# Two busiest experts in groups of 32 rows, token lists made at the second layers, projection weights in wider parts

## The chip, the cores and the metric

The kernel runs on one core of one Trainium2 chip. The metric is the time of one execution in microseconds of device time, given as the median of several runs.

## What is computed

Two transformer blocks follow each other on 256 tokens of width 1024, in fp32. The first has a mixer (convolution and two kinds of attention) and a mixture of 32 experts, of which each token goes to 4. The second has two layers of attention and feed-forward over the same tokens and a context of 256 more. The change lies in the experts and in how projection weights are loaded everywhere. The experts' part of the reference:

```python
logits = (xt @ router_w + router_b).astype(jnp.float32)
top_vals, top_idx = lax.top_k(logits, TOP_K)
top_w = jax.nn.softmax(top_vals, axis=-1)
combine = jnp.einsum('tk,tke->et', top_w, one_hot(top_idx, N_EXPERTS))

def expert_step(acc, params):
    w1, b1, w2, b2, gate_e = params
    u = xt @ w1 + b1
    glu = jnp.minimum(u[:, ::2], SWIGLU_LIMIT)
    lin = jnp.clip(u[:, 1::2], -SWIGLU_LIMIT, SWIGLU_LIMIT)
    a = glu * jax.nn.sigmoid(SWIGLU_ALPHA * glu) * (lin + 1)
    out = a @ w2 + b2
    return acc + gate_e[:, None] * out, None
```

## The kernel before

The program has three stages: the first block's mixer (0 to 266 us in the profile), the experts (to about 1597 us), and the latent layers of the second block. While the experts run, a second stream of work, the *side stream*, is fed in between: the layers of the second block that need only the context. `along` gives it credit at each step of an expert; `SHARE` says how much, by the expert's size.

The experts are sorted by their number of tokens and run in that order. Each has a fixed room (`CAPS`): 128 rows for the two busiest (ranks 0 and 1), 64 for ranks 2 to 17, 32 for the rest. What does not fit would be done in a loop at the end. From rank 2 on, the first layer of the next expert stands ahead of the second layer of this one. An expert does the following.

- Its tokens are gathered by matmuls with a 0/1 matrix (`held`, `inward`, L858).
- `first` (bias L887 or L889, matmuls L899) multiplies the tokens by 8 weight pieces of 1 MB (`m_raw`, from `in_w_mlp` on SP's queue, five buffers). For 128 rows each 512 columns are done as two tiles of 64 rows, for 64 rows as one, for 32 rows as one of 32; such tiles run side by side on the array.
- `act` (L909 to L916) is the gated activation, a chain that alternates between VectorE (DVE) and ScalarE (ACT), in the tiles `glu` and `sg`, which have one buffer each. `across` (L924) transposes its result, and ScalarE copies it to `aT`.
- `second` (L957) multiplies by 4 more pieces. `halved` (L966, L967) scales the result by each row's gate and splits it in a high and a low part.
- `scatter` (L1007) brings the rows back to their tokens: matmuls with `selT`, a 0/1 matrix made from the expert's token list, added to the output on VectorE (`add`, L981). One scatter serves one expert of 128 rows, or a pair of smaller ones.

The lists of tokens and gates of all 32 experts are made before the first scatter by `ranked`, in 16 rounds of two experts. A round compares each token's place in the expert with the row number (L789, two operations on VectorE), multiplies by token number and gate (L794, four matmuls), and puts the result in `lists` and `gates` (L796 to L799).

All other projections go through `Weights` with `w_raw`, `w_hi`, `w_lo`. A piece of 2048 columns is loaded in `PIECES` parts. ScalarE rounds a part to `w_hi` (L96); VectorE or GpSimd (POOL) subtracts to get `w_lo` (L98): GpSimd takes each sixth part in the first mixer, all beside the experts, and each second in the latent layers (`POOL_EVERY`); then three matmuls (L195, L196, L197) use them. `LEAD` is how many parts are split ahead, `LAG` by how many parts loading trails the splitting. Beside the experts the ACT queue loads these parts, in the latent layers the SP queue does (both by L113).

## Time and profile before

| | |
|---|---|
| Time, median of 3 runs | 2373.54 us (2371.75 to 2374.51) |
| Profiled execution | 2361.89 us, span 2360.2 us, mean granted clock 0.957 |
| TensorE (PE) busy | 2137.9 us, 91% of the span |
| VectorE (DVE) busy | 1135.5 us, 48% |
| ScalarE (ACT) busy | 892.8 us, 38% |
| GpSimd (POOL) busy | 625.1 us, 26% |
| DMA | 667.5 MB, mean 283 GB/s |
| Experts' weights | 384 pieces of 1 MB on SP's queue, median 8.1 us from issue to landing |

The shares are averages over three stages that differ. In the page's 40 slices the DMA engines are at nine tenths or more for most of the experts' stage, and TensorE in the latent layers and at the start of the experts. So a stretch is to be read before an average.

### The profile page before, as it was taken

The page shows a single profiled execution, that of the slowest core. Times are in us where ns is not written, and L with a number is a line of the kernel's source. Part 1 is how long each engine was busy: PE and PEld are TensorE (multiplying, and loading weights), DVE is VectorE, ACT ScalarE, POOL GpSimd, SP SyncE. Part 2 cuts the span into 40 slices and gives each one's busy share as a digit, 9 for nine tenths or more (in the row PEclk, how much of TensorE's full clock was granted, in tenths as well). Part 3 has the DMA queues.
Part 4 walks back from the last instruction along what each step waited for, and adds up shares of the span by engine and source line. Part 5 has one row for each costly group of instructions (what it writes and reads, how often), then busy time and mean ns, then how long its engine had stood idle before and what let it go on. Part 6 is the DMA issues. An engine that isn't in the chain of part 4 may idle for free. (4 is left out here: it accounts for less than half of the span.)

```text
span 2360.2 us, 40173 instructions
## 1 busy us (share of the span) xinstructions
PE 2137.9 (91%) x15186; PEld 1500.9 (64%) x15187; DVE 1135.5 (48%) x2305; ACT 892.8 (38%) x1912; POOL 625.1 (26%) x540
## 2 busy tenths in 40 slices
PE   6899899999999888977989898878999999899998
PEld 3667534555444432525766665637789998788997
DVE  4766343121334222324342345227669988767555
ACT  2444301232332111214433333314555446566554
POOL 0001200122001000203544343404224454323442
PEclk6999899999999999988999999978999999999999
DMA  7867856899988999998999999994246855233663
GB/s 295 331 244 270 317 207 238 337 380 364 353 322 324 338 379 426 377 405 329 360 387 373 377 389 380 365 400 136 81 148 233 305 191 171 86 108 110 196 183 99
DMA packets 168967, 667.49 MB, mean 283 GB/s; under 512 B 20192, under 2 KB 22112, under 8 KB 110016
## 3 DMA queue, kind: packets, MB, share of 16 engines
q1 hardware_dynamic: 135696, 597.87, 67.8%
q10 hardware_dynamic: 33072, 66.99, 8.2%
q8 instruction: 121, 1.98, 0.3%
q14 instruction: 78, 0.64, 0.1%
HBM read 661.51 MB, written 3.28 MB: 282 GB/s over the span
## 5 line engine op out<-in xcount | busy, mean ns | idle before, releaser
L98 POOL TENSOR_TENSOR w_lo<-w_raw,w_hi 128x512 fp32r<-128x512 f32 x417 | 563.9, 1361 | 1175.6 <-ACT w_hi L96 1016.4
L96 ACT ACTIVATE w_hi<-w_raw 128x512 fp32r<-128x512 f32 (+1 forms) x660 | 398.4, 623 | 347.2 <-PE c L196 145.0
L899 PE MATMUL u<-m_raw,xT 128*64 128x512 f32 (+1 forms) x2048 | 401.9, 629 | 45.5 <-DMA m_raw<-in_w_mlp 45.5
L195 PE MATMUL ps<-uh,w_hi 128*128 128x256 f32 (+1 forms) x944 | 273.1, 290 | 13.0 <-ACT uh L1209 9.1
L196 PE MATMUL ps<-ul,w_hi 128*128 128x256 f32 (+1 forms) x944 | 269.9, 286 | 0.8 <-DVE ul L1210 0.6
L197 PE MATMUL ps<-uh,w_lo 128*128 128x256 f32 (+1 forms) x944 | 269.1, 285 | 0.2 <-DVE w_lo L98 0.2
L98 DVE TENSOR_TENSOR w_lo<-w_raw,w_hi 128x512 fp32r<-128x512 f32 (+1 forms) x243 | 200.4, 831 | 116.9 <-ACT w_hi L96 94.7
L899 PEld LDWEIGHTS u<-m_raw,xT 128*64 128x64 f32 (+1 forms) x2048 | 104.5, 127 | 238.5 <-issue 171.5
L957 PE MATMUL y<-m_raw,aT 128*32 128x256 f32 (+1 forms) x1536 | 210.8, 496 | 14.2 <-DMA m_raw<-in_w_mlp 13.6
L195 PEld LDWEIGHTS ps<-uh,w_hi 128*128 128x128 f32 (+1 forms) x944 | 181.1, 192 | 20.3 <-ACT uh L1209 10.3
L196 PEld LDWEIGHTS ps<-ul,w_hi 128*128 128x128 f32 (+1 forms) x944 | 182.0, 193 | 2.4 <-DVE ul L1210 1.5
L197 PEld LDWEIGHTS ps<-uh,w_lo 128*128 128x128 f32 (+1 forms) x944 | 182.0, 193 | 0.6 <-DVE w_lo L98 0.4
L195 PE MATMUL c<-uh,w_hi 128*128 128x256 f32 (+1 forms) x584 | 170.3, 292 | 10.6 <-DVE sg L1568 3.5
L196 PE MATMUL c<-ul,w_hi 128*128 128x256 f32 (+1 forms) x584 | 169.5, 290 | 0.7 <-DVE ul L1210 0.7
L197 PE MATMUL c<-uh,w_lo 128*128 128x256 f32 (+1 forms) x584 | 169.8, 291 | 0.0
L197 PE MATMUL ps<-hh,w_lo 128*128 128x256 f32 x560 | 160.5, 287 | 5.5 <-DVE w_lo L98 5.5
L195 PE MATMUL ps<-hh,w_hi 128*128 128x256 f32 x560 | 163.7, 292 | 0.2 <-ACT hh L188 0.2
L196 PE MATMUL ps<-hl,w_hi 128*128 128x256 f32 x560 | 159.2, 284 | 0.1
L957 PEld LDWEIGHTS y<-m_raw,aT 128*32 128x32 f32 (+1 forms) x1536 | 73.0, 126 | 121.7 <-issue 85.0
L195 PEld LDWEIGHTS c<-uh,w_hi 128*128 128x128 f32 (+1 forms) x584 | 111.5, 191 | 28.1 <-issue 12.9
L909 DVE TENSOR_SCALAR glu<-u 128x512 f32<-128x512 f32 (+1 forms) x34 | 23.4, 688 | 220.1 <-PE u L899 220.0
L196 PEld LDWEIGHTS c<-ul,w_hi 128*128 128x128 f32 (+1 forms) x584 | 111.6, 191 | 15.0 <-issue 11.0
(549 smaller groups left out, 3928.4 us busy)
## 6 DMA issues: line engine op xcount, KB each, us to landing
m_raw<-in_w_mlp SPq DMA_DIRECT2D x384, 1024.0 KB, 8.1
f_raw<-in_w_ada SPq DMA_DIRECT2D x47, 1024.0 KB, 7.7
w_raw<-in_w_ffn_in SPq DMA_DIRECT2D x176, 256.0 KB, 3.7
w_raw<-in_w_in SPq DMA_DIRECT2D x128, 256.0 KB, 4.0
w_raw<-in_w_ffn_in ACTq DMA_DIRECT2D x88, 256.0 KB, 8.1
w_raw<-in_w_ffn_out SPq DMA_DIRECT2D x88, 256.0 KB, 3.6
w_raw<-in_w_in ACTq DMA_DIRECT2D x68, 256.0 KB, 7.8
g_raw<-in_w_ada SPq DMA_DIRECT2D x16, 1024.0 KB, 7.7
```

The costliest lines, as they stand in the source:

```text
L96: nc.scalar.activation(hi, r, AF.Copy)
L98: e.tensor_tensor(lo, r, hi.bitcast(F32), op=ALU.subtract)
L195: nc.tensor.matmul(out, lh, rh, start=start, stop=False)
L196: nc.tensor.matmul(out, lh, rl, start=False, stop=False)
L197: nc.tensor.matmul(out, ll, rh, start=False, stop=stop)
L899: nc.tensor.matmul(u[z][r:r + s], xT[:, k, x0:x0 + s], ws[k - k0][:, c * 512:(c + 1) * 512], start=False, stop=k == KC - 2)
L909: nc.vector.tensor_scalar(glu, u0, 7.0, None, op0=ALU.min)
L957: nc.tensor.matmul(y[z][r:r + s], a[:, k], ws[(k - k0) // 2][:, k % 2 * D + c * wd:k % 2 * D + (c + 1) * wd], start=k == 3, stop=k == 4)
```

## The change

It has three parts.

1. The two busiest experts get room for 96 rows, as three groups of 32. `first` runs 12 tiles of 32 rows where it ran 8 of 64, `second` 12 of 32 rows and 256 columns where it ran 4 of 64 rows and 512, `inner` three activation chains on 64 partitions where it ran two on 128, and two chained scatters take the place of one (48 matmuls for 16).
2. The lists are no longer made in advance. `listed` makes them when a second layer begins: for one busiest expert in two calls, for others once for a pair. It uses a tile that shares its one buffer with `glu`, and what is still open of the last scatter is finished first (`self.all(behind)`).
3. Projection weights come in 2 parts of 1024 columns (512 KB) where there were 4 of 512 (256 KB), with `LEAD` and `LAG` set to match. `POOL_EVERY` is the same number of parts, and so twice the columns. The credit of the side stream is set anew for the three sizes.

```text
first L899 -> L901   second L957 -> L960   transposes L924 -> L926   scatter L1007 -> L1012
lists L794 -> L860   bias L887, L889 -> L891   split w_hi L96, w_lo L98 -> L97, L99   projections L195 to L197 -> L196 to L198
```

```diff
-PIECES = 4
-LEAD = 3
-LAG = 2
+PIECES = 2
+LEAD = 2
+LAG = 1
 POOL_EVERY = 6, 2
 
 
-SHARE = {128: 0.8, 64: 1.45, 32: 3.2}
+SHARE = {96: 0.6, 64: 1.5, 32: 3.2}
 DRY = 2.0
...
-CAPS = ((0, 2), 128), ((2, 18), 64), ((18, 32), 32)
+CAPS = ((0, 2), 96), ((2, 18), 64), ((18, 32), 32)
...
-        yield
-        lists, gates = keep["lists"], keep["gates"]
-        n = 2
-        for a in range(0, NE, n):
-            b, m = a + n, CAP[a]
-            pt = ps.tile([P, 512], F32, name="m")
-
-            rows = p2.tile([P, 2, 2, P], F32R, name="rows2", tag="sg", bufs=1)
-            for t in range(2):
-                nc.vector.tensor_tensor(rows[:, t].rearrange("p e (d m) -> p e d m", m=m),
-                                        keep["place"][:, 0:m].rearrange("p (e d m) -> p e d m", e=1, d=1).to_broadcast([P, n, P // m, m]),
-                                        slot[:, t, a:b].rearrange("p (e d m) -> p e d m", d=1, m=1).to_broadcast([P, n, P // m, m]), op=ALU.is_equal)
-            for e in range(n):
-                for t in range(2):
-                    nc.tensor.matmul(pt[:, 4 * e:4 * e + 4], rows[:, t, e], val[:, t, a + e], start=t == 0, stop=t == 1)
-            v = pt[:, 0:4 * n].rearrange("p (e n) -> p e n", n=4)
-            nc.vector.tensor_scalar(lists[:, a:b], v[:, :, 0], -1.0, None, op0=ALU.add)
-            low = p.tile([P, 4], F32, name="low", bufs=2)[:, 0:n]
-            nc.vector.tensor_copy(low, v[:, :, 2])
-            nc.vector.tensor_tensor(gates[:, a:b], v[:, :, 1], low, op=ALU.add)
...
-            for n, shape, dt in (("rslot", [P, 2, NE], F32), ("rgate", [P, 2, NE], F32), ("lists", [P, NE], F32), ("gates", [P, NE], F32), ("place", [P, T], F32)):
+            keep["rslot"], keep["rgate"] = keep["slot"], keep["gate"]
+            for n, shape, dt in (("val", [P, 2, NE, 4], F32R), ("place", [P, T], F32)):
...
+            def listed(subs):
+
+
+                n = len(subs)
+                rows = p2.tile([P, 2, 2, P], F32R, name="rows2", tag="glu", bufs=1)
+                pt = ps.tile([P, 512], F32, name="m")
+                for e, (slot, a, m, what) in enumerate(subs):
+                    for t in range(2):
+                        nc.vector.tensor_scalar(rows[:, t, e].rearrange("p (d m) -> p d m", m=m),
+                                                keep["place"][:, a:a + m].rearrange("p (d m) -> p d m", d=1).to_broadcast([P, P // m, m]),
+                                                slot(t), None, op0=ALU.is_equal)
+                for e, (slot, a, m, what) in enumerate(subs):
+                    for t in range(2):
+                        nc.tensor.matmul(pt[:, 4 * e:4 * e + 4], rows[:, t, e], what(t), start=t == 0, stop=t == 1)
+                v = pt[:, 0:4 * n].rearrange("p (e n) -> p n e", n=4)
+                lg = p2.tile([P, 3, 2], F32, name="lg")[:, :, 0:n]
+                nc.vector.tensor_copy(lg[:, 1:3], v[:, 1:3])
+                nc.vector.tensor_scalar(lg[:, 0], v[:, 0], -1.0, None, op0=ALU.add)
+                nc.vector.tensor_tensor(lg[:, 1], lg[:, 1], lg[:, 2], op=ALU.add)
+                return [(lg[:, 0, e:e + 1], lg[:, 1, e:e + 1]) for e in range(n)]
+
+            def groups(r):
+
+                at = lambda z: (lambda t: z[:, t, r])
+                m = 64 if CAP[r] == 64 else 32
+                slot = lambda t: keep["rslot"][:, t, r:r + 1]
+                return [(slot, a, m, at(keep["val"])) for a in range(0, CAP[r], m)]
...
-                n = 128 // m
-                u = [ps.tile([P, 512], F32, name="u" if c < 2 else "y") for c in range(max(1, 4 // n))]
-                for v in range(2):
-                    if m == 128:
-                        for b in range(2):
-                            q = slice(64 * b, 64 * b + 64)
-                            nc.tensor.matmul(u[2 * v + b], bl[0][q], b1h[q, v], start=True, stop=False, tile_position=(64 * b, 0))
-                    else:
-                        nc.tensor.matmul(u[v if m == 64 else 0], bl[v], b1h[:, v], start=m == 64 or v == 0, stop=False)
-
-                tiles = [(c, h, h, c) for c in range(4) for h in (0, 64)] if m == 128 else [(c // n, c % n * m, 0, c) for c in range(4)]
-                s = min(m, 64)
+                n = m // 32
+                u = [ps.tile([P, 512], F32, name="u" if z < 2 else "y") for z in range(n)]
+                for z in range(n):
+                    for v in (z,) if m == 64 else range(2):
+                        nc.tensor.matmul(u[z], bl[v], b1h[:, v], start=m == 64 or v == 0, stop=False)
+
+                s = 64 if m == 64 else 32
+                tiles = [(c // 2, c % 2 * 64, 0, c) for c in range(4)] if m == 64 else [(z, 32 * c, 32 * z, c) for z in range(n) for c in range(4)]
...
-                if m == 128:
+                def turned(sg, aT):
+                    nc.scalar.activation(aT.rearrange("p (b i) r -> p i b r", b=2), across(sg).rearrange("p i (b r) -> p i b r", b=2), AF.Copy)
+
+                if m == 96:
                     aT = [p2.tile([P, KC, 64], F32, name="aT") for _ in range(2)]
-                    for b in range(2):
-                        pt = across(act(u[b], u[2 + b]))
-                        for h in range(2):
-                            nc.scalar.activation(aT[h][:, 4 * b:4 * b + 4], pt[:, :, 64 * h:64 * h + 64], AF.Copy)
+                    aT = [aT[z // 2][:, :, z % 2 * 32:z % 2 * 32 + 32] for z in range(3)]
+                    for z, a in zip(u, aT):
+                        turned(act(z[0:64], z[64:128]), a)
                     return aT
...
             def second(m, aT):
 
-                n = 4 if m == 32 else 2
+                n, s = (2, 64) if m == 64 else (4, 32)
                 wd = D // n
-                y = [ps.tile([P, 512], F32, name="y")[:, 0:wd] for _ in aT]
-                s = min(m, 64)
+                banks = [ps.tile([P, 512], F32, name="y") for _ in range((len(aT) + 1) // 2)]
+                y = [banks[z // 2][:, z % 2 * wd:(z % 2 + 1) * wd] for z in range(len(aT))]
                 for k0 in range(0, KC, 4):
                     ws = w.some(2)
                     with tc.manual_schedule(engines={mybir.EngineType.PE}):
                         for k in reversed(range(k0, k0 + 4)):
-                            for c in range(n):
-                                for h, a in enumerate(aT):
-                                    z, r = (c, 64 * h) if m == 128 else (0, c * s)
-                                    nc.tensor.matmul(y[z][r:r + s], a[:, k], ws[(k - k0) // 2][:, k % 2 * D + c * wd:k % 2 * D + (c + 1) * wd],
-                                                     start=k == 3, stop=k == 4)
+                            for z, a in enumerate(aT):
+                                for c in range(n):
+
+                                    nc.tensor.matmul(y[z][c * s:(c + 1) * s], a[:, k], ws[(k - k0) // 2][:, k % 2 * D + c * wd:k % 2 * D + (c + 1) * wd],
...
-            def scatter(m, ys, selTs):
-
...
+            def scatter(m, ys, lists):
+
+                selTs = [tokens(z) for z in lists]
+                per = 2 if m == 32 else 4
...
-                        for n in range(2 * len(selTs)):
-                            selT, z = selTs[n // 2], n % 2
+                        for n in range(2 * len(ys)):
+                            z = n % 2
...
-                                b, c = k // per, slice(k % per * P, (k % per + 1) * P)
-                                y, r = (ys[b], 0) if m == 128 else (ys[n // 2], b * s)
-                                nc.tensor.matmul(po[q][:, i * T:(i + 1) * T], y[z][r:r + s, c], selT[r:r + s],
-                                                 start=n == 0, stop=n == 2 * len(selTs) - 1, tile_position=(r, 0))
+                                r, c = slice(k // per * m, (k // per + 1) * m), slice(k % per * P, (k % per + 1) * P)
+                                nc.tensor.matmul(po[q][:, i * T:(i + 1) * T], ys[n // 2][z][r, c], selTs[n // 2][r],
+                                                 start=n == 0, stop=n == 2 * len(ys) - 1, tile_position=(k // per * m, 0))
...
             for n, (r, layer) in enumerate(order):
-                m, ranks = CAP[r], UNITS[unit[r]]
-                run = first(m, ready[r], chosen(m, perm[:, r:r + 1])) if layer == 1 else second(m, aTs.pop(r))
+                m = CAP[r]
+                if layer == 1:
+                    run = first(m, ready[r], chosen(m, perm[:, r:r + 1]))
+                else:
+                    self.all(behind)
+                    if m == 96:
+                        lg = [z for i in (0, 2) for z in listed(groups(r)[i:i + 2])]
+                    elif r % 2 == 0:
+                        lg = listed(groups(r) + groups(r + 1))
+                    run = second(m, aTs.pop(r))
...
                 else:
-                    gate = keep["gates"][:, r:r + 1]
-                    if m == 32:
-                        e = ranks.index(r)
-                        if e % 2 == 0:
-                            both = [p2.tile([P, 512], F32R, name=z) for z in ("yh", "yl")]
-                        ys[r] = halved(got[0], gate, [z[:, e % 2 * T:e % 2 * T + T] for z in both])
+                    if m == 96:
+                        out = [halves() for _ in range(2)]
+                        y = [halved(z, lg[i][1], [o[:, i % 2 * T:i % 2 * T + T] for o in out[i // 2]]) for i, z in enumerate(got)]
+                        behind = chain(*(scatter(32, y[i:i + 2], [z for z, _ in lg[i:i + 2]]) for i in (0, 2)))
                     else:
-                        ys[r] = [halved(y, gate) for y in got]
-                    if m == 128 or r % 2:
-                        self.all(behind)
-                        rs = (r,) if m == 128 else (r - 1, r)
-                        y = ys[r] if m == 128 else [ys[z] if m == 32 else ys[z][0] for z in rs]
-                        behind = scatter(m, y, [tokens(keep["lists"][:, z:z + 1]) for z in rs])
+                        if m == 64 or r % 2 == 0:
+                            out = halves()
+                        o = out if m == 64 else [z[:, r % 2 * T:r % 2 * T + T] for z in out]
+                        ys[r] = halved(got[0], lg[r % 2][1], o)
+                        if r % 2:
+                            behind = scatter(m, [ys[r - 1], ys[r]], [z for z, _ in lg])
```

The loop for rows that do not fit is changed to pieces of 64 rows; it is not shown.

The order on TensorE at the start of the first expert's first layer, before (`L899` is the layer, `L794` the lists):

```order
L887 MATMUL u<-b1h,bl 128x512
L887 MATMUL y<-b1h,bl 128x512 x2
L899 MATMUL u<-m_raw,xT 64x512 x3
L794 MATMUL m<-val,rows_2544 128x4 x4
L899 MATMUL u<-m_raw,xT 64x512
L899 MATMUL y<-m_raw,xT 64x512
L794 MATMUL m<-val,rows_2556 128x4
L899 MATMUL y<-m_raw,xT 64x512 x2
L794 MATMUL m<-val,rows_2556 128x4 x3
L899 MATMUL y<-m_raw,xT 64x512
```

and with the change (`L901` is the layer, `L995` the second layers' biases):

```order
L891 MATMUL u<-b1h,bl 128x512 x4
L891 MATMUL y<-b1h,bl 128x512 x2
L901 MATMUL u<-m_raw,xT 32x512 x8
L901 MATMUL y<-m_raw,xT 32x512 x4
L901 MATMUL u<-m_raw,xT 32x512 x8
L901 MATMUL y<-m_raw,xT 32x512 x4
L995 MATMUL m<-gateT,b_2253 128x256 x4
L901 MATMUL u<-m_raw,xT 32x512 x8
```

The list matmuls between the layer's own are gone; there are three tiles (two called u and one y) with four matmuls each.

The order on TensorE at the end of that expert's first layer, before (`L242` and `L252` are side work, `L924` the transposes that end a chain, `L957` the second layer):

```order
L242 MATMUL c<-f_raw,sc_254 32x512 x13
L924 MATMUL m<-ident,sg 128x128 x4
L887 MATMUL u<-b1h,bl 128x512
L242 MATMUL c<-f_raw,sc_254 32x512 x3
L957 MATMUL y<-m_raw,aT 64x512 x2
L242 MATMUL c<-f_raw,sc_254 32x512 x4
L252 MATMUL c<-ident,ada 128x128 x4
L957 MATMUL y<-m_raw,aT 64x512
L924 MATMUL m<-ident,sg 128x128 x4
L957 MATMUL y<-m_raw,aT 64x512 x29
```

and with the change (`L243`, `L253` side work, `L926` transposes, `L960` the second layer, `L860` the lists):

```order
L243 MATMUL c<-f_raw,sc_258 32x512 x2
L926 MATMUL m<-ident,sg 128x64 x4
L243 MATMUL c<-f_raw,sc_258 32x512 x3
L960 MATMUL y<-m_raw,aT 32x256 x4
L243 MATMUL c<-f_raw,sc_258 32x512 x4
L253 MATMUL c<-ident,ada 128x128 x4
L891 MATMUL u<-b1h,bl 128x512 x2
L926 MATMUL m<-ident,sg 128x64 x4
L960 MATMUL y<-m_raw,aT 32x256 x4
L926 MATMUL m<-ident,sg 128x64 x4
L860 MATMUL m<-val,rows_2588 128x4 x4
L960 MATMUL y<-m_raw,aT 32x256
```

Three chains end where two did, with the same side matmuls among them, and the lists stand after the third.

The order on TensorE at the second layer of the expert of rank 2, before:

```order
L195 MATMUL c<-uh,w_hi 128x256
L957 MATMUL y<-m_raw,aT 64x512 x8
L924 MATMUL m<-ident,sg 128x128 x4
L889 MATMUL u<-b1h,bl 128x512
L196 MATMUL c<-ul,w_hi 128x256
```

and with the change:

```order
L198 MATMUL c<-uh,w_lo 128x256
L960 MATMUL y<-m_raw,aT 64x512 x5
L860 MATMUL m<-val,rows_3687 128x4 x4
L960 MATMUL y<-m_raw,aT 64x512 x3
L926 MATMUL m<-ident,sg 128x128 x4
L891 MATMUL u<-b1h,bl 128x512
```

The four list matmuls of ranks 2 and 3 now stand after the fifth of eight matmuls of the second layer, ahead of the transposes.

## Rows read from the trace of the kernel before

**Rows 1.** Stretches: length, busy us of each engine, granted clock, DMA share, GB/s
```profile
290.00:338.00 48.00, 48.00 (x208) 18.70 (x208) 19.40 (x89) 2.53 (x5) 1.27 (x1) 1.00 0.62 221
424.00:600.00 176.00, 174.10 (x1000) 96.44 (x996) 35.96 (x70) 50.45 (x95) 47.18 (x37) 1.00 0.98 373
600.00:780.00 180.00, 169.85 (x934) 79.20 (x934) 77.08 (x210) 50.46 (x129) 8.75 (x16) 1.00 0.90 330
780.00:1080.00 300.00, 254.38 (x1386) 110.56 (x1386) 74.33 (x162) 51.38 (x91) 27.20 (x27) 0.94 0.96 385
1080.00:1560.00 480.00, 428.90 (x3598) 311.78 (x3599) 186.23 (x352) 179.01 (x367) 206.38 (x160) 0.95 0.96 373
1780.00:1980.00 200.00, 192.57 (x1575) 188.70 (x1573) 181.31 (x258) 107.26 (x235) 99.26 (x70) 1.00 0.69 234
2160.00:2340.00 180.00, 180.00 (x1508) 180.00 (x1507) 105.62 (x165) 104.30 (x220) 83.83 (x62) 1.00 0.56 170
```

**Rows 2.** Groups by form on PE, 290 to 424 us: busy us, mean ns | idle
```profile
L794 PE MATMUL m<-val,rows 128*128 128x4 f32 x64 | 12.1, 261 | 0.0
...
L1007 PE MATMUL m<-selT,yh 128*128 128x256 f32 x8 | 1.8, 309 | 0.0
```

**Rows 3.** Timeline of PE: start us, length us, instruction
```profile
1160.17 1.93 PE L957 MATMUL y<-m_raw,aT 128*32 128x256 f32 x32
...
1166.48 1.92 PE L899 MATMUL u<-m_raw,xT 128*32 128x512 f32 x16
```

**Rows 4.** Timeline of PE and DVE at two pairs of experts
```profile
473.26 3.65 PE L957 MATMUL y<-m_raw,aT 128*64 128x512 f32 x16
...
474.79 0.69 DVE L916 SCALAR_TENSOR_TENSOR sg<-sg,glu 128x512 f32<-128x512 f32 x1
...
713.09 3.65 PE L957 MATMUL y<-m_raw,aT 128*64 128x512 f32 x16
...
715.62 0.69 DVE L916 SCALAR_TENSOR_TENSOR sg<-sg,glu 128x512 f32<-128x512 f32 x1
```

**Rows 5.** Timeline of PE: transposes that end the activation chains of both busiest experts
```profile
342.23 0.66 PE L924 MATMUL m<-ident,sg 128*128 128x128 f32 x4
...
348.62 0.66 PE L924 MATMUL m<-ident,sg 128*128 128x128 f32 x4
...
397.20 0.66 PE L924 MATMUL m<-ident,sg 128*128 128x128 f32 x4
...
406.18 0.66 PE L924 MATMUL m<-ident,sg 128*128 128x128 f32 x4 [0.53 <-DVE sg L916]
```

**Rows 6.** Groups by form on DVE, 337 to 424 us
```profile
L845 DVE TENSOR_SCALAR rows<-place,rslot 128x64 fp32r<-128x64 f32 x8 | 1.4, 252 | 0.0
```

**Rows 7.** The page's part 3: queue, packets, MB, share of 16 engines' span
```profile
q1 hardware_dynamic: 135696, 597.87, 67.8%
q10 hardware_dynamic: 33072, 66.99, 8.2%
```

**Rows 8.** Timeline of DVE, first latent feed-forward
```profile
1842.18 1.38 DVE L98 TENSOR_TENSOR w_lo<-w_raw,w_hi 128x512 fp32r<-128x512 f32 x1 [0.42 <-ACT w_hi L96]
...
1846.60 0.68 DVE L98 TENSOR_TENSOR w_lo<-w_raw,w_hi 128x512 fp32r<-128x512 f32 x1
1847.20 0.42 DVE L189 TENSOR_TENSOR hl<-sg,hh 128x256 fp32r<-128x256 f32 x1
```

**Rows 9.** Groups by form on DVE, 1780 to 1980 us
```profile
L98 DVE TENSOR_TENSOR w_lo<-w_raw,w_hi 128x512 fp32r<-128x512 f32 x66 | 64.7, 987 | 5.4 <-ACT w_hi L96 5.4
```

**Rows 10.** Waits of SP's queue, 1080 to 1560 us: us in total, times, longest
```profile
SPq L113 <- DMA w_raw<-in_w_ffn_in: 146.1, 26, 10.5
```

**Rows 11.** Timeline of POOL beside rows 8
```profile
1841.71 3.01 POOL L98 TENSOR_TENSOR w_lo<-w_raw,w_hi 128x512 fp32r<-128x512 f32 x2 [0.83 <-ACT w_hi L96]
1847.73 4.25 POOL L98 TENSOR_TENSOR w_lo<-w_raw,w_hi 128x512 fp32r<-128x512 f32 x3 [3.02 <-ACT w_hi L96]
1858.71 1.37 POOL L98 TENSOR_TENSOR w_lo<-w_raw,w_hi 128x512 fp32r<-128x512 f32 x1 [6.74 <-ACT w_hi L96]
```

More of the change, by code (lines that the diff above doesn't have):

```diff
@@ L1065, in experts @@
                     yield step
-                if layer == 1 and n + 1 < len(order) and CAP[r] > 32 and CAP[next((z for z, v in order[n + 1:] if v == 1), 0)] == 32:
-                    nc.vector.tensor_scalar(bl, keep["place"][:, 0:192], 0.0, None, op0=ALU.mult)
                 if layer == 1:
+                    if m > 32 and CAP[next((z for z, v in order[n + 1:] if v == 1), 0)] == 32:
+                        nc.vector.tensor_scalar(bl, keep["place"][:, 0:192], 0.0, None, op0=ALU.mult)
                     inside[r] = inner(m, got)
-                    if m == 128:
+                    if m == 96:
                         aTs[r] = end(inside.pop(r))
@@ L1132, in experts @@
                             for t in range(2):
-                                nc.vector.tensor_scalar(rows[:, t], place[:, v], col[:, t:t + 1], None, op0=ALU.is_equal)
-                                nc.scalar.activation(held_r[:, t], rows[:, t], AF.Copy)
-                                nc.vector.tensor_copy(val[:, t, 0:1], tok[:, t:t + 1])
+                                nc.vector.tensor_scalar(held_r[:, t], place[:, v], col[:, t:t + 1], None, op0=ALU.is_equal)
+                                for i in (0, 3):
+                                    nc.vector.tensor_copy(val[:, t, i:i + 1], tok[:, t:t + 1])
@@ L1142, in experts @@
+                            ((tokens_of, gate),) = listed([(lambda t: col[:, t:t + 1], 64 * v, 64, lambda t: val[:, t])])
+                            xT = pf.tile([P, KC, 64], F32, name="xTf")
                             inward(held_r, xT)
-                            u = end(first(128, xT, chosen(128, col[:, 4:5])))
-                            y = end(second(128, end(inner(128, u))))
-                            self.all(scatter(128, [halved(z, lg[:, 1:2]) for z in y], [tokens(lg[:, 0:1])]))
+                            u = end(first(64, xT, chosen(64, col[:, 4:5])))
@@ L1146, in experts @@
+                            y = end(second(64, end(inner(64, u))))
+                            self.all(scatter(64, [halved(y[0], gate, halves())], [tokens_of]))
                             after()
```

61 lines of the change are left out of this document (26 added, 35 removed).

## The prediction

> **What bounds the kernel now.** I read the table of stretches first [rows 1]. Up to 780 us TensorE is the bound: it works 48.0 of 48 us in the first layer of the first expert, 174.1 of 176 us from 424 on and 169.9 of 180 us after that. From 780 to 1560 the experts' weights are: the 16 DMA engines are busy for 0.96 of the time, while TensorE stands still for 45.6 of 300 and 51.1 of 480 us. In the latent layers TensorE is full again (180.0 of 180 us in the last stretch), with VectorE close to its end in one of them (181.3 of 200 us). So work taken off TensorE counts one for one before 780 us and in the latent layers, and between those only fewer or better-fed transfers count.
>
> Then the groups by form tell what the matmuls cost [rows 2], and the timeline of TensorE what they cost when they stand in one run [rows 3, 4]. The trace shows two instructions for each fp32 matmul of the experts. In the rows a run of sixteen 64-row instructions of 512 columns takes 3.65 us, 0.228 each; sixteen 32-row ones take 1.92 us, 0.120 each; thirty-two 32-row ones of 256 columns take 1.93 us, 0.060 each. Half the rows, half the price for each.
>
> **The sum, step by step**, against the profiled execution's 2361.9 us.
>
> *The lists leave the first layer.* The 64 list matmuls took 12.1 us of a TensorE that never paused [rows 1, 2]: −12.1.
>
> *First and second layers of the two busiest experts.* First layer: 128 instructions × 0.228 = 29.2 us become 192 × 0.120 = 23.0, −6.2 each. Second layer: 64 × 0.228 = 14.6 us become 192 × 0.060 = 11.5, −3.1 each. Twice that: −18.6.
>
> *Their scatters.* 16 matmuls become 48, so 32 more for each expert. Packed closely a 256-column matmul costs 180 / 1508 = 0.119 us [rows 1]; a scatter's own group shows 1.8 / 8 = 0.225 [rows 2]. That is 7.6 to 14.4 us for both experts. I take 8, since a chained scatter is a long run. The eight more additions of each lie on VectorE, which is half idle there.
>
> *The third activation chain.* Each group of rows has its own chain of min, exponentials and products on one buffer, so the three run one after the other. Their ends can be seen as the transposes: 342.23 and 348.62, then 397.20 and 406.18 us [rows 5], 6.4 and 9.0 us apart. A chain on half as many partitions has the same columns, so I price it the same. If nothing covers the third chain it costs 15.4, if side matmuls fill it, 0. The order lists 51 more matmuls of the side stream before the end of the second expert's second layer than before (133 against 82); at 0.119 they give back 6.1. I take 15.4 − 6.1 = +9.3.
>
> *The lists come back at the second layers.* A busiest expert has 6 list matmuls, at 12.1 / 64 = 0.19 [rows 2] 1.1 us, and a wait for its rows that no row prices: nothing if they are early, about 3 us if both calls wait like the pairs below; I take 1.5, so 5.2 for two experts. For a pair of 64-row experts the order puts four list matmuls after the fifth of eight second-layer matmuls. They need four row-making operations of 0.25 us [rows 6], in the buffer that the activation chain frees with its last operation. In [rows 4] that one ends at 474.79 + 0.69 = 475.48; with 4 × 0.25 the rows are there at 476.5 at the earliest, but TensorE reaches the lists after 5/8 of the run of 3.65 us that starts at 473.26, at 475.5. It would wait 1.0 us in a place where it now goes on. The second pair of rows there, worked in the same way, gives 715.62 + 0.69 + 1.0 − 713.09 − 2.28 = 1.9, and a pair whose chain ends early gives 0: these are my bounds. Five pairs lie in the stretches with a full TensorE: 5 × (4 × 0.19 + 1.0) = 8.8. The other ten lie where it waits for weights anyway and are costed at nothing; that cover is the 45.6 + 51.1 us of [rows 1]. Sum +14.0 (bounds 6 to 22).
>
> *Transfers in parts of 512 KB.* The ACT queue carried 66.99 MB in 8.2% of 2360.2 us, 2.889 us per MB; the SP queue, mostly 1 MB pieces, 2.677 [rows 7]. If the larger parts reached the price of the SP queue, 66.99 × 0.212 = 14.2 us of the 16 engines' time would be saved, nearly all of it where they are the limit. They are only doubled, and part of that queue is other traffic: bounds 0 and −14.2, and I take the middle, −7.
>
> *Half as many splits.* VectorE takes 0.68 us for a 512-column subtraction that nothing disturbs and 0.42 for one of 256 [rows 8], so 1024 columns come to 0.42 + 3 × 0.26 = 1.20 instead of 1.36. In the stretch where VectorE is nearly full it makes 66 of them [rows 9]: 33 × 0.16 = 5.3. Some of that is not on the path: −3 (0 to −5). The halves on ScalarE and GpSimd save as little and are hidden elsewhere.
>
> Together −12.1 − 18.6 + 8 + 9.3 + 14.0 − 7 − 3 = −9.4. So the experts themselves come out about even (+0.6), and the forecast hangs on the transfers and splits. The median of the runs shown, 2373.5, lies 11.6 us above the profiled execution; the difference is put on the median: **2364 us**. By the bounds that I hold likely this case lies between 2352 and 2376. 0.2% is 4.7 us, about what a measurement of this kernel can tell from no change.
>
> **Rivals.**
>
> *The lists hold up TensorE at every pair (slower).* The rows of a list share one buffer with the activation chain, so the list waits for the chain and the next chain for the list's matmuls. At the dear end, 1.9 us, each of the 15 pairs costs 1.9 + 0.76 = 2.66 us, 39.9 in place of 8.8. With half of the 31 us hidden in the idle time between 780 and 1560 that is +16: about **2380**. For it: the order stands the lists in the middle of the second layers, on an engine that takes its work in order. Against it: where I could work it out the first early pair waits half as long. It turns the sign once lists and waits cost over 14.0 + 9.4 = 23.4 us in all.
>
> *The transfers were hidden (no change).* If the small parts of the ACT queue only fill gaps between the experts' pieces, the −7 go and +0.6 − 3 are left: about **2371**. For it: the DMA engines are already at 0.96, so little more fits there.
>
> *Fewer issues feed the DMA engines better (faster still).* SP, which issues the experts' weights, stood 146.1 us waiting for one kind of projection part to land between 1080 and 1560 [rows 10], and the experts' next weights stand behind that wait on its queue. If half as many parts close the gap from 0.96 to 1.00 there, 0.04 × 480 = 19 us go: about **2345**. Against it: the engines may be busy for 0.96 because the rest is the turn from one transfer to the next.
>
> *A longer GpSimd piece blocks VectorE (slower).* In [rows 8] the same subtraction takes VectorE 1.38 us at 1842.18 and 0.68 us at 1846.60. By [rows 11] GpSimd was working during the first and not during the second, and one of its pieces takes 1.37 us. With pieces twice as long, 1.37 us more would be lost where VectorE runs into one, say at half of the 22 steps of a feed-forward layer: 15 us if none is hidden, so about **2379**. The total of GpSimd's work doesn't grow, and TensorE is ahead in most of that stretch, so I hold it unlikely. The Trainium skill ("SBUF — State Buffer", section "SBUF: two separate sides") says that the port pair these two engines share is an exclusive lock: a VectorE operation with two SBUF inputs and a GpSimd operation exclude each other for the whole instruction, and the loser is fully blocked. By that rule the trace agrees (1.38 against 0.68 us), and the wider parts would cost this price wherever the two meet.
>
> That the change does not do what it says (the busiest experts overflowing 96 rows, and the loop for the rest being entered) I leave out: the reference's router, with its own inputs, gives the busiest experts 80 and 66 tokens, and every other one no more than its 64 or 32.
>
> **How the numbers follow.** The forecast has 0.45: 0.30 of it below 2368.8 (0.2% under 2373.5), 0.15 within 0.2%. The rivals have 0.22 (lists, slower), 0.11 (hidden, no change), 0.17 (better fed, faster) and 0.05 (blocked, slower). Faster: 0.30 + 0.17 = 0.47. No change: 0.15 + 0.11 = 0.26. Slower: 0.22 + 0.05 = 0.27. The range of 2340 to 2389 takes in the faster rival with 5 us to spare for the bounds of the other terms, and the list rival with 9.
>
> **What would show it.** Step by step: no list matmuls in the first expert's first layer, which is 18 us shorter; second-layer runs of 32-row matmuls at 0.060; three transposes 6 to 9 us apart, with TensorE idle or on side work between them; waits of TensorE for the rows of lists of up to 1.9 us at the early pairs, and none that matter after 780; the ACT queue at less than 2.889 us per MB; VectorE below 181 us in the stretch of the first latent feed-forward. It is wrong if the time moves in the latent layers by more than 5 us, if the transfers between 780 and 1560 end over 10 us earlier than the experts' own start explains, or if the lists' waits go on past 780.

## The result, and the profile after

| | before | after |
|---|---|---|
| Median | 2372.6 us (4 runs) | 2407.1 us (2401.3 to 2413.2, 4 runs) |
| Profiled execution | 2361.9 us | 2413.2 us, span 2411.4, granted clock 0.941 |

The change made the kernel slower: ratio 1.0142, 95% interval 1.0114 to 1.0171, +34 us. The forecast was 2364 (2340 to 2389). Runs of one kernel lie up to 12 us apart here (up to 22 in the experiments), and the profiled execution after was among its slow ones and the one before among its fast ones; so the two traces differ by 51 us where the medians differ by 34.

The table of stretches after the change (the columns are those of [rows 1]):

```profile
290.00:338.00 48.00, 43.50 (x333) 17.81 (x333) 14.66 (x33) 8.95 (x16) 1.85 (x4) 0.93 0.80 315
424.00:600.00 176.00, 173.24 (x996) 93.40 (x990) 46.92 (x95) 46.01 (x77) 40.19 (x17) 1.00 0.95 368
600.00:780.00 180.00, 171.09 (x937) 78.45 (x933) 77.00 (x216) 48.57 (x124) 6.09 (x14) 1.00 0.89 330
780.00:1080.00 300.00, 255.10 (x1360) 113.01 (x1361) 83.73 (x205) 50.02 (x82) 26.48 (x15) 0.95 0.95 376
1080.00:1560.00 480.00, 432.92 (x3470) 319.81 (x3469) 218.49 (x373) 163.06 (x278) 184.75 (x83) 0.92 0.91 352
1780.00:1980.00 200.00, 181.60 (x1457) 174.52 (x1456) 160.69 (x236) 94.84 (x166) 76.95 (x32) 0.97 0.64 225
```

TensorE has idle time in the first expert that it did not have (43.5 of 48 us), the DMA engines fall from 0.96 to 0.91 between 1080 and 1560, and the granted clock there from 0.95 to 0.92. From the timelines, the end of the second layer of some ranks (us from the start):

```text
end of second layer, rank    1      12      16      27      31   first layer of rank 0 from   end of span   from rank 31 to the end
before                     424.0   872.4  1006.1  1470.2  1597.0            290.0                2360.2              763.2
after                      424.8   873.8  1016.9  1508.1  1631.5            298.3                2411.4              780.0
```

The mixer ends 8 us later, the two busiest experts give that back, ranks 2 to 12 take as long as before. Then 33 us are lost between ranks 12 and 31, and 17 in the latent layers.

The first expert in TensorE's timeline (start, length, instruction):

```profile
298.35 1.92 PE L901 MATMUL u<-m_raw,xT 128*32 128x512 f32 x16
300.09 1.04 PE L901 MATMUL y<-m_raw,xT 128*32 128x512 f32 x8
...
327.95 0.46 PE L926 MATMUL m<-ident,sg 64*128 64x64 f32 x4
...
336.39 0.69 PE L926 MATMUL m<-ident,sg 64*128 64x64 f32 x4
...
342.10 0.66 PE L926 MATMUL m<-ident,sg 64*128 64x64 f32 x4 [3.46 <-DVE sg L918]
...
345.13 10.54 PE L960 MATMUL y<-m_raw,aT 128*32 128x256 f32 x171
```

These answer to [rows 3, 5]: sixteen 32-row matmuls in 1.92 us, 171 of the second layer in 10.54 (0.062 each), no lists between them, and three transposes 8.4 and 5.7 us apart. So the first part does what the sum says.

The queues (the columns are those of [rows 7]):

```profile
q1 hardware_dynamic: 104016, 597.86, 65.5%
q10 hardware_dynamic: 17520, 66.99, 7.6%
```

The ACT queue now costs 7.6% of 2411.4 us for its 66.99 MB, 2.74 us per MB (2.89 before). The transfers have become cheaper, and the DMA engines stand still more.

### The profile page after: what moved, and what is told of

It is laid out like the page before. It is cut to its first block, busy times and chain, and to the rows that moved or that the text cites. A ratio compares the mean times of both kernels' runs of the same rounds, so it can differ in the third digit from the quotient of the medians.

```text
span 2411.4 us, 39292 instructions
## 1 busy us (share of the span) xinstructions
PE 2165.8 (90%) x15654; PEld 1538.9 (64%) x15655; DVE 1185.3 (49%) x2267; ACT 856.2 (36%) x1590; POOL 569.3 (24%) x333
## 3 DMA queue, kind: packets, MB, share of 16 engines
q10 hardware_dynamic: 17520, 66.99, 7.6%
## 5 line engine op out<-in xcount | busy, mean ns | idle before, releaser
L98 POOL TENSOR_TENSOR w_lo<-w_raw,w_hi 128x1024 fp32r<-128x1024 f32 x210 | 506.4, 2414 | 1205.2 <-ACT w_hi L96 957.4
L96 ACT ACTIVATE w_hi<-w_raw 128x1024 fp32r<-128x1024 f32 (+1 forms) x332 | 343.9, 1045 | 322.6 <-PE c L197 154.7
L901 PE MATMUL u<-m_raw,xT 128*32 128x512 f32 (+1 forms) x2176 | 386.3, 620 | 30.0 <-DMA m_raw<-in_w_mlp 30.0
L901 PEld LDWEIGHTS u<-m_raw,xT 128*32 128x32 f32 (+1 forms) x2176 | 102.6, 125 | 230.9 <-issue 176.8
L960 PE MATMUL y<-m_raw,aT 128*32 128x256 f32 (+1 forms) x1792 | 222.9, 483 | 12.0 <-DMA m_raw<-in_w_mlp 11.6
L98 DVE TENSOR_TENSOR w_lo<-w_raw,w_hi 128x1024 fp32r<-128x1024 f32 (+1 forms) x122 | 152.6, 1253 | 88.5 <-ACT w_hi L96 86.6
L960 PEld LDWEIGHTS y<-m_raw,aT 128*32 128x32 f32 (+1 forms) x1792 | 78.5, 127 | 112.0 <-issue 71.2
L214 DVE TENSOR_SCALAR sg<-sg 128x256 f32<-128x256 f32 x66 | 83.3, 1264 | 98.2 <-ACT sg L213 97.5
```

The lines of the kernel that those rows point to most:

```text
L96: nc.scalar.activation(hi, r, AF.Copy)
L98: e.tensor_tensor(lo, r, hi.bitcast(F32), op=ALU.subtract)
L214: nc.vector.tensor_scalar(out, out, 1e38, None, op0=ALU.min)
L901: nc.tensor.matmul(u[z][r:r + s], xT[:, k, x0:x0 + s], ws[k - k0][:, c * 512:(c + 1) * 512], start=False, stop=k == KC - 2)
L960: nc.tensor.matmul(y[z][c * s:(c + 1) * s], a[:, k], ws[(k - k0) // 2][:, k % 2 * D + c * wd:k % 2 * D + (c + 1) * wd], start=k == 3 and z ...
```

## The experiments

Medians below are of each kernel's own runs; a ratio is to the kernel before, run beside it on the same chip, with its 95% interval. All edits are to the changed kernel unless it says otherwise.

**One part undone or alone.** Narrow parts again:

```diff
-PIECES = 2
-LEAD = 2
-LAG = 1
+PIECES = 4
+LEAD = 3
+LAG = 2
```

> The changed kernel with its third part undone: PIECES 4, LEAD 3, LAG 2, the rest kept. Theory A (the wider parts cost the time: a part of 1024 columns is rounded and subtracted in one piece, so TensorE and the loads wait longer between ranks 16 and 27 and in the latent layers, and TensorE's clock falls in those gaps): nearly all of it comes back, about 2365 to 2373 us, and the second layer of rank 27 ends within 5 us of before's 1470. Theory B (the lists at the second layers stop TensorE at the late pairs, where the trace shows waits for list rows of 11.2 us between 1080 and 1560): the loss stays, 2395 to 2405 us.

2367.5 us, ratio 0.9997 (0.9970 to 1.0024). The groups and the lists together change nothing that can be told from no change; the third part is the whole loss. One sign of theory A did not come: the second layer of rank 27 ended at 1480.7 us, 10 later than before and not within 5.

The reverse edit in the kernel before:

> The kernel before with the third part alone: PIECES 2, LEAD 2, LAG 1. Theory A: slower than before by most of the loss, 2395 to 2410 us, with the DMA engines' share under 0.93 between 1080 and 1560 where it was 0.96. Theory B: within 0.3% of before, 2365 to 2378 us.

2402.3 us, 1.0121 (1.0085 to 1.0157). The third part alone makes nearly the whole loss, as theory A says; the DMA engines' share between 1080 and 1560 fell to 0.94 only, less than I had expected of it.

More parts ahead (`LEAD = 3`, `LAG = 2`, parts of 1024):

> The changed kernel with LEAD 3 and LAG 2 in place of 2 and 1, the parts still 1024 columns. Theory A in the form that too few parts are split ahead: most of the loss comes back, 2375 to 2385 us. Theory A in the form that one part takes too long from landing to use, whatever is ahead: no change, 2400 to 2410 us. Theory B: no change, 2400 to 2410 us.

2407.3 us, 1.0139 (1.0103 to 1.0175). How far ahead the splitting runs is not the matter.

The groups alone, lists in advance (`listed` called for all experts ahead of the loop, results kept in a tile of their own), narrow parts:

> The first part alone: three groups of 32 rows for the two busiest experts, lists made in advance in the first layer as before (in 17 calls, each with its own place for the result), PIECES 4, LEAD 3, LAG 2. By my sum the first part is worth -18.6 + 8 + 9.3 = -1.3 us, so 2365 to 2373 us; Theory B: as before, with e1 slower than this by 25 us or more; Theory A: e1 and this within 8 us of each other.

2385.8 us, 1.0051 (1.0026 to 1.0075). Neither bound was met, and it does not price the first part: making the lists in advance takes 72 comparisons on VectorE here (19 rounds, not the 17 that I had expected) where the kernel before makes 32, and the first expert's second layer ended at 378.4 us (362.3 before). Behind the two busiest experts it is clean, though. From the end of rank 1 to the end of rank 31 it took 1173.1 us, the kernel before 1173.0, and the one with lists at the second layers and narrow parts 1191.1. By these single traces the lists at the second layers cost 18 us over the 15 pairs, 1.2 each.

**Loads and splits taken apart.** The third part widens two things at once: the transfer, and the operations that split what it brings. First wide loads with narrow splits: `PIECES`, `LEAD` and `LAG` are as before, and one transfer of 1024 columns fills a tile that is split in two parts.

```diff
-        while self.loaded < min(len(self.order), free + self.raws):
...
+        while self.halves and self.loaded < len(self.order) and self.loaded + self.joined[self.loaded] <= free + self.raws:
+            k = self.joined[self.loaded]
+            t = self.pool.tile([P, 2 * self.width], F32, name=f"{self.name}_raw", bufs=self.raws // 2)
+            n = self.order[self.loaded][0].shape[-1]
+            self.queue.dma_start(t[:, :k * n], self.whole[self.loaded])
+            for z in range(k):
+                self.parts[self.loaded] = t[:, z * n:(z + 1) * n]
+                self.loaded += 1
```

> The changed kernel with loads of 1024 columns, but split and handed on in parts of 512 (LEAD 3, LAG 2, eight halves as before; four raw tiles of 1024). Theory L (the loads: one wide transfer lands later than the first of two narrow ones and frees its buffer later): the loss stays, 2395 to 2410 us. Theory S (the splits: one operation on 1024 columns, on ScalarE and then VectorE or GpSimd, keeps the next stage and its neighbours waiting): the loss is gone, 2362 to 2372 us.

2347.5 us, 0.9893 (0.9862 to 0.9923): not only is the loss gone, the loads bring 20 us. Then the opposite, two transfers into one wide part:

```diff
-            self.queue.dma_start(t[:, :n], src)
+            for c in range(0, n, 512) if self.halves else (0,):
+                self.queue.dma_start(t[:, c:min(c + 512, n)] if self.halves else t[:, :n], src[:, c:min(c + 512, n)] if self.halves else src)
```

> The changed kernel with each 1024-column part loaded by two transfers of 512 columns, split in one piece as in the change. Theory L: the loss shrinks by more than half, under 2388 us. Theory S: the loss stays, 2400 to 2412 us.

2436.7 us, 1.0247 (1.0208 to 1.0287): worse than either. Theory L falls, and theory S says too little: the change was a gain and a larger loss in one.

**Which split.** All tiles and loads stay 1024 wide, and the operations are cut. All of them:

```diff
-                nc.scalar.activation(hi, r, AF.Copy)
                 e = nc.gpsimd if (self.cut + 1) % self.pool_every == 0 else nc.vector
-                e.tensor_tensor(lo, r, hi.bitcast(F32), op=ALU.subtract)
+                for z in range(0, n, 512):
+                    c = slice(z, min(z + 512, n))
+                    nc.scalar.activation(hi[:, c], r[:, c], AF.Copy)
+                    e.tensor_tensor(lo[:, c], r[:, c], hi[:, c].bitcast(F32), op=ALU.subtract)
```

> The changed kernel with rounding and subtraction both done as two operations of 512 columns each; the tiles (w_raw, w_hi, w_lo), and with them when a buffer comes free, and the loads stay 1024 wide. If the length of the operations is the cause: 2365 to 2378 us. If the size in which buffers are handed on is: 2395 to 2410 us.

2354.1 us, 0.9922 (0.9897 to 0.9947). The length of the operations is the cause, not the size of the buffers; that this lies 7 us above the kernel with wide loads and narrow splits is within the intervals. The three further edits cut the loop above to one engine or one step. GpSimd's subtraction alone:

> The changed kernel with GpSimd's subtraction of each part done as two operations of 512 columns; ScalarE's rounding, VectorE's subtractions, tiles and loads stay 1024 wide. Theory S in the form that GpSimd's longer piece holds up VectorE (its min before the feed-forward's logarithm takes 1264 ns on average with the change, 933 before): that mean falls back below 1000 ns and most of the loss is gone, 2365 to 2380 us. Theory S in the form that the whole chain of a part is longer: less than a third comes back, 2395 to 2405 us. Theory L: nothing comes back.

2393.2 us, 1.0068 (1.0044 to 1.0092): 14 of 53 us, between the two forecasts. ScalarE's rounding alone:

> The changed kernel with ScalarE's rounding alone done as two operations of 512 columns; the subtractions stay 1024 wide and wait for both. The halves of GpSimd alone gave back 14 of the 53 us that all halves gave back (2407 to 2393, and to 2354). If ScalarE's longer operation holds up the work queued behind it on ScalarE: a third or more comes back, 2375 to 2390 us. If only the subtractions count, or only that the second stage can begin after the first half: 2400 to 2410 us.

2386.9 us, 1.0055 (1.0031 to 1.0079): 20 us. The subtractions on both engines:

> The changed kernel with the subtractions on both engines done as two operations of 512 columns; the rounding stays 1024 wide. If the subtractions' length is the cause (VectorE's own and what GpSimd's blocks of VectorE): 2354 to 2368 us, like all halves. If the handing on of the first half to the next stage matters most: 2385 to 2395 us, no better than GpSimd's halves alone.

2379.1 us, 1.0022 (1.0002 to 1.0041): 28 us, between the two forecasts. Rounding and subtractions add up: 20 + 28 = 48 of 53, each uncertain by some 6 us by its interval. There is no single culprit. By the traces GpSimd's share lies beside the experts: with its halves alone the time from the end of rank 1 to the end of rank 31 goes from 1206.7 to 1194.0 us, and the latent layers from 780.0 to 778.4 only. Rounding alone and both subtractions alone bring the latent layers to 769.0 and 769.4.

How GpSimd's share comes about can be read. Groups on VectorE between 1090 and 1590 us, where GpSimd makes all subtractions (busy us, mean ns of one), before:

```profile
L1474 DVE TENSOR_TENSOR acc<-acc,c 128x512 f32<-128x512 f32 x40 | 27.4, 684 | 29.6 <-PE c L197 29.5
...
L213 DVE TENSOR_SCALAR sg<-sg 128x256 f32<-128x256 f32 x22 | 16.0, 729 | 65.8 <-ACT sg L212 65.7
L189 DVE TENSOR_TENSOR hl<-sg,hh 128x256 fp32r<-128x256 f32 x22 | 12.2, 552 | 15.1 <-ACT hh L188 14.9
L914 DVE TENSOR_TENSOR glu<-glu,sg 64x512 f32<-64x512 f32 x12 | 12.1, 1008 | 12.6 <-ACT sg L913 12.6
```

after:

```profile
L214 DVE TENSOR_SCALAR sg<-sg 128x256 f32<-128x256 f32 x22 | 30.1, 1368 | 78.8 <-ACT sg L213 78.8
L1480 DVE TENSOR_TENSOR acc<-acc,c 128x512 f32<-128x512 f32 x40 | 27.3, 684 | 25.1 <-PE c L198 25.0
...
L190 DVE TENSOR_TENSOR hl<-sg,hh 128x256 fp32r<-128x256 f32 x22 | 18.1, 825 | 7.5 <-ACT hh L189 7.4
L916 DVE TENSOR_TENSOR glu<-glu,sg 64x512 f32<-64x512 f32 x11 | 14.3, 1296 | 12.0 <-ACT sg L915 12.0
```

and with GpSimd's subtraction in halves:

```profile
L1482 DVE TENSOR_TENSOR acc<-acc,c 128x512 f32<-128x512 f32 x40 | 27.3, 682 | 21.5 <-PE c L200 21.5
...
L216 DVE TENSOR_SCALAR sg<-sg 128x256 f32<-128x256 f32 x22 | 17.0, 775 | 82.1 <-ACT sg L215 82.1
L192 DVE TENSOR_TENSOR hl<-sg,hh 128x256 fp32r<-128x256 f32 x22 | 12.8, 580 | 9.7 <-ACT hh L191 9.7
L918 DVE TENSOR_TENSOR glu<-glu,sg 64x512 f32<-64x512 f32 x11 | 11.3, 1025 | 15.2 <-ACT sg L917 15.2
```

The min (L213, L214, L216) goes from 729 ns to 1368 and back to 775; the product of two tiles in SBUF (L914, L916, L918) from 1008 to 1296 and back to 1025; the addition from PSUM (L1474, L1480, L1482) stays at 682 to 684. These means mix two cases. Single mins of the trace after, and the GpSimd piece beside the second:

```profile
1187.84 0.29 DVE L214 TENSOR_SCALAR sg<-sg 128x256 f32<-128x256 f32 x1 [9.59 <-ACT sg L213]
...
1197.40 2.32 DVE L214 TENSOR_SCALAR sg<-sg 128x256 f32<-128x256 f32 x1 [4.84 <-ACT sg L213]
...
1197.23 2.34 POOL L98 TENSOR_TENSOR w_lo<-w_raw,w_hi 128x1024 fp32r<-128x1024 f32 x1 [1.66 <-ACT w_hi L96]
```

A min that meets no subtraction of GpSimd takes 0.28 to 0.30 us, before and after; one that meets a piece ends just behind it. Of the 22 mins in the stretch 12 meet one in either kernel; these take 1.10 us on average before and 2.27 after. So GpSimd's piece of 2.41 us in place of 1.36 holds up VectorE where both work in SBUF. The Trainium skill ("SBUF — State Buffer", section "SBUF: two separate sides") says of their shared port pair that whoever starts first has it for the whole instruction, if VectorE's operation has two inputs in SBUF or is in a two-port mode. The rows of the product and of the addition agree (1008 to 1296 ns, and 684 both times); the min, with one input, is held up too, and that it is in such a mode no run here shows. But the mean of the min is no measure of the time. With rounding alone in halves it is at 474 ns in that stretch, with GpSimd's pieces still whole, because only 3 of 22 mins meet one; with wide loads and narrow splits, the fast kernel, it is at 1073 ns, because 19 of 22 meet a short one.

Cutting an operation does a second thing: the engine that waits for it can begin when the first half is done. With both subtractions in halves it does:

```profile
1831.74 0.69 DVE L100 TENSOR_TENSOR w_lo<-w_raw,w_hi 128x512 fp32r<-128x512 f32 x1
...
1832.48 0.39 PE L200 MATMUL ps<-hh,w_lo 128*128 128x256 f32 x1 [0.53 <-DVE w_lo L100]
1832.54 0.69 DVE L100 TENSOR_TENSOR w_lo<-w_raw,w_hi 128x512 fp32r<-128x512 f32 x1
```

TensorE goes on after the first half, before the second has begun. How the 28 us of the subtractions divide between this and shorter pieces in the way of other work was not separated. The 20 us of the rounding cannot come from it: the subtraction still waits for both halves, and no wait of TensorE in the trace after is put down to `w_hi`.

What TensorE sees of the longer pieces are the waits, between 1090 and 1590 us (us in total, times, longest), after:

```profile
PE c L196 <- DVE acc L1480: 13.3, 8, 3.8
PE m L860 <- DVE rows L855: 11.2, 5, 4.0
PE u L891 <- DVE sg L917: 7.2, 5, 3.1
```

with all splits in halves:

```profile
PE m L862 <- DVE rows L857: 8.4, 7, 2.6
PE c L198 <- DVE acc L1482: 7.0, 5, 2.7
...
PE u L893 <- DVE sg L919: 1.7, 2, 1.5
```

and the stretch as a whole (columns of [rows 1]), before:

```profile
1090.00:1590.00 500.00, 441.71 (x3713) 314.82 (x3713) 183.56 (x343) 177.87 (x364) 204.75 (x157) 0.94 0.97 375
```

after:

```profile
1090.00:1590.00 500.00, 448.91 (x3596) 328.72 (x3596) 217.69 (x367) 164.65 (x280) 190.41 (x80) 0.91 0.92 356
```

with all splits in halves:

```profile
1090.00:1590.00 500.00, 452.43 (x3751) 317.41 (x3749) 189.14 (x390) 167.70 (x351) 201.44 (x156) 0.93 0.96 380
```

with wide loads and narrow splits:

```profile
1090.00:1590.00 500.00, 453.36 (x3793) 321.72 (x3785) 207.42 (x394) 176.40 (x357) 204.17 (x157) 0.95 0.96 383
```

In the last three TensorE is busy for the same 449 to 453 us, yet after the change it gets through 3596 instructions where the others do 3751 and 3793, at a granted clock of 0.91 against 0.93 and 0.95. So it hardly stands still for longer (51 us of the 500, against 48 and 47; before it was 58). More of its pauses are on VectorE, though (31.7 us in these three kinds, 17.1 with the halves), and its clock is low for more of the time. The trace grants two levels, 1.0 and 0.5 (2.4 and 1.2 GHz); an average of 0.91 means 90 of the 500 us at the lower one, 0.95 means 50. A fall of the clock, after the change:

```profile
1258.00:1263.00 5.00, 5.00 (x59) 3.94 (x58) 1.61 (x2) 2.73 (x4) 2.88 (x2) 1.00 1.00 359
1266.00:1272.00 6.00, 4.57 (x21) 4.31 (x22) 3.38 (x11) 1.10 (x3) 1.29 (x1) 0.50 1.01 417
1273.00:1300.00 27.00, 25.96 (x230) 20.05 (x229) 10.76 (x13) 8.93 (x13) 13.31 (x6) 1.00 0.79 308
```

From 1263.43 to 1267.43 TensorE waits 4.0 us for list rows; the clock falls in that wait and is back at 1273. How much of the loss is the pauses and how much the clock was not separated. In the latent layers, waits for `w_lo`, after:

```profile
PE ps L198 <- DVE w_lo L98: 8.5, 6, 1.4
...
PE ps L198 <- POOL w_lo L98: 5.3, 6, 2.7
```

and with all splits in halves:

```profile
PE ps L200 <- DVE w_lo L100: 1.8, 4, 0.6
```

13.8 us became 1.8; these layers take 780.0 and 761.1 us. One such wait, after the change, on all engines (start, length):

```profile
1818.74 6.28 POOL L1544 TENSOR_TENSOR ss<-vec,mod 128x8 f32<-128x8 f32 x1 [15.29 <-DVE ul L1216]
...
1825.30 2.35 POOL L98 TENSOR_TENSOR w_lo<-w_raw,w_hi 128x1024 fp32r<-128x1024 f32 x1
1825.36 2.64 DVE L214 TENSOR_SCALAR sg<-sg 128x256 f32<-128x256 f32 x2 [0.41 <-ACT sg L213]
...
1827.70 0.39 PE L198 MATMUL ps<-uh,w_lo 128*128 128x256 f32 x1 [2.67 <-POOL w_lo L98]
```

A small operation of GpSimd (128x8) takes 6.28 us from 1818.74 on, in which VectorE is at work for 6.22; GpSimd's subtraction of the next part follows at 1825.30 and lasts 2.35; VectorE's min has started at 1825.36, two of them in 2.64, which ends behind that piece; and TensorE has stood for 2.67 us when the part is there at 1827.70.

**What the good half is worth, and the lists.** Wide loads and narrow splits in the kernel before (the edit of the wide loads, nothing else):

> The kernel before with wide loads and narrow splits alone (128 rows, lists in advance). With the changed groups and lists the same step took 2367 to 2347.5 us. If the wide loads are worth the same here: 2350 to 2355 us, and the changed groups and lists are then worth under 6 us together, as in the comparison of narrow parts (ratio 0.9997). If the groups and lists only pay once the transfers are no longer the bound: 2360 to 2368 us, 12 us or more above the same with the changed groups and lists.

2338.1 us, 0.9850 (0.9816 to 0.9884), faster than both forecasts. The load alone brings 36 us there, against 20 with the new groups and lists, which with wide loads seem to cost 9 us (the intervals just overlap). Between the ends of ranks 1 and 31, where the lists come back, this kernel takes 1143.8 us, and with the new groups and lists 1168.7. So the last kernel has the wide loads, the groups, and the rows of the lists in another buffer:

```diff
-                rows = p2.tile([P, 2, 2, P], F32R, name="rows2", tag="glu", bufs=1)
+                rows = p2.tile([P, 2, 2, P], F32R, name="rows2", tag="yl")
```

> The changed kernel with loads of 1024 and splits of 512 columns (2347.5 us), and the rows of the lists no longer in the activation's buffer but in the ring of the scatter's low halves, which is free earlier. Comparing lists in advance with lists at the second layers (both with narrow parts), the pairs from rank 2 on took 18 us more with the latter. If the shared buffer makes the lists late: the waits of TensorE for list rows (7.6 us from 414 us on with the shared buffer) fall under 2 us and 8 to 18 us come back, 2330 to 2340 us. If the lists' own matmuls and the extra work on VectorE are what costs: under 5 us come back, 2343 to 2348 us.

2332.0 us, 0.9831 (0.9804 to 0.9858): faster than both kernels, 15.5 us from this one line. The waits for list rows between 414 and 1600 us with the shared buffer:

```profile
PE m L873 <- DVE rows L868: 7.6, 10, 1.6
```

and with the other ring:

```profile
PE m L873 <- DVE rows L868: 0.6, 1, 0.6
```

Between the ends of ranks 1 and 31 it takes 1142.8 us, no more than with lists in advance. It helps by more than these 7.0 us. The next activation chain no longer has to wait for the lists' matmuls to let go of the buffer, and the order now places them between other work; which of these brings the rest was not separated.

## Why the prediction was wrong, step by step

- **Half as many splits** is the step that failed. It had one engine's saving of fixed cost in it (−3, bounds −5 and 0), with the halves on ScalarE and GpSimd "hidden elsewhere". Cutting the operations again takes the time from 2407 to 2354: the term is +53. I counted how long the engines work and not how long each piece stands between its neighbours: a part now takes 1.05 + 2.41 us through ScalarE and GpSimd where it took 0.62 + 1.36, what is queued behind a piece waits nearly twice as long, and the saving is lost in that. The upper bound of 0 had no row behind it: none showed that a longer operation could cost no time.
- **The rival of the longer GpSimd piece** had that mechanism, and a price of 15 us; the halves of GpSimd alone brought 14. That the numbers agree is luck. I looked for it in the latent feed-forward alone, and there the halves bring 1.6 us; the rest came beside the experts, where I had priced nothing. I gave it 0.05, because the total of GpSimd's work does not grow. ScalarE's and VectorE's own pieces cost most of the other 39.
- **Transfers of 512 KB** were mis-sized: −7 (0 to −14.2), measured −20 with the new groups (2367.5 to 2347.5) and −36 without. With wide loads and narrow splits the queues cost

```profile
q1 hardware_dynamic: 104016, 597.86, 67.0%
q10 hardware_dynamic: 17520, 66.99, 7.6%
```

  which is 74.6% of 2347.3 = 1751 us of the engines' time against 76.0% of 2360.2 = 1794 in [rows 7]: 43 us, three times my bound. I had priced only the ACT queue, and SP's queue carries 392 such parts too. But SP's parts do not explain the time, since nearly all of them belong to the mixer and the latent layers, and the latent layers took 766.5 us with narrow and 764.5 with wide loads. The gain lies between the ends of ranks 1 and 31 (1191.1 to 1168.7 us, and 1173.0 to 1143.8 in the kernel before). There the ACT queue, between 424 and 1590 us with narrow parts and with wide loads, costs

```profile
q10 hardware_dynamic: 29232, 52.97, 13.6%
...
q10 hardware_dynamic: 14688, 52.70, 12.0%
```

  which is 19 us less of 1166. So the saving on the ACT queue alone is above my upper bound, and what brings the rest of these 22 and 29 us stays open. The rival of better-fed DMA engines (−19) had the right sign for this half; the gap that it wanted closed shrank in part, from 0.96 to 0.97 between 1080 and 1560, and to 0.98 in the kernel before.
- **Lists at the pairs** were priced 8.8 us, for the five early pairs only; measured 18 over all fifteen with narrow parts and 25 with wide loads (1143.8 to 1168.7), and with a buffer of their own nothing is left of it (1142.8). The ten late ones were not free: with narrow parts TensorE still waits 8.8 us for list rows between 780 and 1600. Why a stretch with the DMA engines at 0.96 passes such waits on, the traces do not settle. The wait itself was right in kind: the trace after has ten of them, 17.0 us from 424 us on. But eight of these, 13.3 us, lie behind 780, where the forecast had none that matter, and the longest is 4.0 where it had 1.9.
- **The two busiest experts** were nearly right. With narrow parts, from the start of the first layer to the end of rank 1 they take 407.0 − 285.5 = 121.5 us, before 424.0 − 290.0 = 134.0: −12.5, where my terms give −12.1 − 18.6 + 8 + 9.3 + 5.2 = −8.2. That the sum of groups and lists, +0.6, agrees with the ratio of 0.9997 is luck in part: the experts came out 4 us better and the pairs 9 dearer, and the interval (−7 to +6 us) takes in either sum.
- The statement that time in the latent layers moving by more than 5 us would refute the forecast was the right alarm: they moved by 17.

## What to carry to other kernels

Choose the size of a transfer and the size of the operations on it separately: the DMA engines gain from the wider transfer, while the engines that pass its content on want pieces short enough not to hold up each other. Before an operation is made longer to save its fixed cost, look at what stands behind it on its own queue and at what it locks out, not only at its busy time. And a wait placed on an engine that takes its work in order is not free because a profile shows that engine idle elsewhere in the stretch.

## What had not been expected of the hardware

Doubling the row that a projection's transfer brings to each partition from 2 to 4 KB went with 43 us less of the 16 DMA engines' time, 2.4% of it, though most of the 667 MB came in unchanged 1 MB pieces. A VectorE operation with one input and a constant (the min) takes 0.29 us alone, but waits out a GpSimd subtraction that is running: 2.32 us beside a piece of 2.34, while additions with an operand in PSUM keep their 684 ns. What was not tried: the first part with lists as cheap as before, the mixer with narrow loads (in single traces it ends about 2 to 11 us later with wide ones), and which operations on ScalarE lose most by its longer rounding.
